# Weight-block sums for ten up-projection units made by DMA in DRAM during the attention, with the signs of the seven products on the token side

## The chip, the cores and the metric

The kernel runs on one core of one Trainium2 chip. The metric is device time in microseconds (us); lower is better. A core has five engines with queues of their own: TensorE (PE in the profile), VectorE (DVE), ScalarE (ACT), GpSimd (POOL) and SyncE (SP), which here only issues DMA transfers. Matrix products are written to PSUM banks; everything else lies in SBUF or in DRAM.

## The reference, cut to what matters

One layer of a diffusion backbone over 1024 tokens of width 1024, with 256 context tokens: modulated RMSNorm, a combined input projection that feeds neighbourhood attention (8 heads) and bidirectional retention (4 heads), gated merge, output projection and residual, and then a gated MLP with a centred convolution over three tokens:

```python
def _conv_ffn(h, w_up, conv_w, conv_b, w_down):
    u = h @ w_up                        # 1024 tokens x 5632 columns
    n = u.shape[1]
    pad = CONV_W // 2
    up = jnp.pad(u, ((0, 0), (pad, pad), (0, 0)))
    u = sum(up[:, i:i + n] * conv_w[i] for i in range(CONV_W)) + conv_b
    a, val = jnp.split(u, 2, axis=-1)
    return (jax.nn.silu(a) * val) @ w_down
```

All inputs, weights and the output are float32.

## The kernel before, in words

**Precision.** Each float32 operand is split in two parts of TensorE's reduced format: ACT copies the high part (`split`, L86), DVE subtracts it to get the low part (L87). A product is three matmuls: high by high, high by low, low by high. A weight block is a [128, 512] tile (256 KB); its two parts go in a `wc` tile, of which there are six.

**Stages**, in order of time: norms and first projections (to about 110 us of the profile), attention (to about 400 us), retention (to about 710 us), gates (to about 870 us), merge, output projection and second norm (to about 1125 us), up projection with convolution (to about 1525 us), down projection.

**Attention.** The loop runs over 34 iterations `i`: 32 units of one head pair and one block of 128 queries, and two to drain. Iteration `i` takes the scores of unit `i` (class `Unit`; its statistics tile `st` has three buffers), the transposes and value products of unit `i-1` and the output of unit `i-2`; between them `piece()` adds PE work from the projections of later pairs and of gates. In each iteration `ada_col2` multiplies one 512 KB block of `w_ada2` with the conditioning vector on DVE (L538); there is one buffer `aw` for it, and the load of the next block (L530) is issued behind that multiplication. That DVE instruction is pinned behind what was traced before it on its engine (`late` is `tc.keep_in_program_order`). POOL has nothing to do in this loop.

**Seven products.** The gates, the up projection and the down projection use a scheme of seven block products in place of eight (class `Seven`). For one block column of the up weights the four blocks are `a11, a12, a21, a22` (rows by column halves of the product's operand), and four sums of them are made on POOL (L1383 to L1386):

```python
pool.tensor_tensor(self.s1, self.a21, self.a22, ALU.add)
pool.tensor_tensor(self.s2, self.s1, self.a11, ALU.subtract)
pool.tensor_tensor(self.s3, self.a11, self.a21, ALU.subtract)
pool.tensor_tensor(self.s4, self.a12, self.s2, ALU.subtract)
```

The token side has four sums of its own, `T1` to `T4`: for the gates in `hx_sums`, for the up projection at the end of `norm_out`, from where they go to DRAM (`d_t`) and come back split in `comb` (tiles `T`). A unit has seven steps of 12 matmuls: `a11` by B11 into bank X, copied by ACT to `p1` (tile `pu`, L1408); `s2` by T2 into Y; `s1` by T1 into Z; `s3` by T3 into Y; `a12` by B21 into X; `a22` by T4 into Y; `s4` by B22 into Z. X and Y are the two halves of one PSUM tile `u`. DVE combines the banks (L1398, L1411, L1417).

**Up projection.** 22 units in the order `seq`; the first two (`PLAIN`) are made with plain products, and the other twenty (class `Up`, numbers 2 to 21) by seven products, each started about three and a half steps after the one before (`interleaved`). Behind every second unit stands the convolution (`conv`), whose result and its sums (tile `sa`, made on POOL, L1777) go to DRAM (`d_a`) for the down projection. The token sums' tiles, the weight blocks (`ur`, L1735) and the weight sums (`s`) share one ring of 12 tiles of [128, 512] (tag `r` of the pool `rp`). `load()` of a unit takes eight of them: four blocks loaded, four sums.

**Order.** The instructions of an engine are ordered when the program is built, by a planner that simulates the engines; each engine then runs its own list in that order and waits on semaphores. So an instruction at the head of an engine's list that waits holds up all behind it, and the order after a change is a new plan. SP's list holds all DMA issues.

Of the kernel before, what the change touches and what calls it, by code (L numbers as in the profile page):

```python
# [8 lines left out]
F32 = mybir.dt.float32  # L9
F32R = mybir.dt.float32r  # L10
AF = mybir.ActivationFunctionType
ALU = mybir.AluOpType
# [4 lines left out]
P = 128  # L17
# [15 lines left out]
NF = FF // P  # L33
# [7 lines left out]
def tile_hybrid_layer(ctx, tc: tile.TileContext, io, dbg=None):  # L41
    nc = tc.nc
    vec, act, pool, pe, sync = nc.vector, nc.scalar, nc.gpsimd, nc.tensor, nc.sync

    def sb(name, side, bufs=1):
        return tc.alloc_tile_pool(name=name, bufs=bufs, side=side, reuse_waits="tile")
# [4 lines left out]
    dram = tc.alloc_tile_pool(name="dram", bufs=1, space=DRAM)  # L51
    d_ona = dram.tile([GR, NJ, 8, NPAIR * P], F32, name="d_ona")
    d_oret = dram.tile([RH * 2, P, T], F32, name="d_oret")
    d_x1 = dram.tile([T, D], F32, name="d_x1")
    d_ada = dram.tile([32, P], F32, name="d_ada")
    d_gate = dram.tile([2 * KB, 2, P, 512], F32, name="d_gate")
    d_pn = dram.tile([KB, 2, P, 512], F32, name="d_pn")
    d_orr = dram.tile([RH * 2, P, T], F32, name="d_orr")
# [6 lines left out]
    cpool = sb("const", "left")  # L65
# [468 lines left out]
    late = tc.keep_in_program_order  # L534
# [6 lines left out]


    dec = cpool.tile([P, RH, 6], F32, name="dec")

    def load_ex():
        cst["lg"] = const("lg", [P, 2, RH])
        cst["ex"] = s0.tile([P, 5], F32, name="ex")
        sync.dma_start(cst["ex"], io["expo"])
# [456 lines left out]
    pieces = filler()  # L1005
# [3 lines left out]
    def piece():  # L1009
        next(pieces, None)  # L1010

    us = []
    for i in range(NPAIR * NJ + 2):
        live = i < NPAIR * NJ
        u1 = us[i - 1] if 1 <= i <= NPAIR * NJ else None
        u2 = us[i - 2] if i >= 2 else None
        if i == 0:
            ada_load()
        for n in (0, 1) if i == 1 else (i,) if 1 < i < 32 else ():
            ada_col2(n)  # L1020
        if u1:
            if u1.j == 0:
                u1.pair.values()
            u1.transp(0)
        piece()
        if u1:
            u1.transp(1)
        if live:
            pair = pairs[i // NJ]
            if i % NJ == 0 and i:  # L1030
                pair.load_bias()
            us.append(Unit(pair, i % NJ))
            us[i].scores()
        if u2:
            u2.output()
        if u1:
            u1.values()
        piece()
        piece()
    for _ in pieces:  # L1040
        pass
    pna.release()
    na.release()
    csp.release()
# [191 lines left out]
    NH = NF // 2  # L1236
# [105 lines left out]
    def hx_sums(k):  # L1342
        b = {}
        for i, half in ((0, 1), (0, 0), (1, 1), (1, 0)):
            kb, c0 = k + KH * i, half * 512
            b[i, half] = t = g_raw("b")
            late(pool.tensor_tensor(t, hxp(0, kb, c0, 512).bitcast(F32), hxp(1, kb, c0, 512).bitcast(F32), ALU.add))
        b11, b12, b21, b22 = b[0, 0], b[0, 1], b[1, 0], b[1, 1]
        for c, o, x, y in (("T1", b11, b12, b11), ("T3", b12, b22, b12), ("T2", b22, b22, b11), ("T4", b21, b21, b22)):
            late(vec.tensor_tensor(o, x, y, ALU.subtract))  # L1350
        yield
        for c, src in (("T2", b22), ("T1", b11), ("T3", b12), ("T4", b21)):
            split(hxT[c][0][:, k], hxT[c][1][:, k], src)
        yield
# [21 lines left out]
    class Seven:  # L1376
        loaded = False

        def load(self):
            self.loaded = True  # L1380
            self.a21, self.a22, self.a11, self.a12 = [self.raw(self.src[b, i]) for b, i in ((1, 0), (1, 1), (0, 0), (0, 1))]
            self.s1, self.s2, self.s3, self.s4 = (self.raw(None) for _ in range(4))
            pool.tensor_tensor(self.s1, self.a21, self.a22, ALU.add)  # L1383
            pool.tensor_tensor(self.s2, self.s1, self.a11, ALU.subtract)
            pool.tensor_tensor(self.s3, self.a11, self.a21, ALU.subtract)
            pool.tensor_tensor(self.s4, self.a12, self.s2, ALU.subtract)  # L1386

        def fetch(self, b, half):
            pass
# [4 lines left out]
            for k, (xh, xl) in enumerate(self.moving(c)):  # L1394
                open3(bank, w[:, 0, k * P : (k + 1) * P], w[:, 1, k * P : (k + 1) * P], xh, xl, first and k == 0, last and k == KH - 1)

        def add(self, b, half, bank, x):
            vec.tensor_tensor(self.dst(b, half), bank, x, ALU.add)  # L1398
            self.done(b, half)

        def step(self, n):
            if n == 0:
                if not self.loaded:
                    self.load()
                self.banks()
                self.p1, self.u2, self.u3 = (self.tmp() for _ in range(3))
                self.prod(self.X, self.a11, "B11", True, False)
                act.copy(self.p1, self.X)  # L1408
            elif n == 1:
                self.prod(self.Y, self.s2, "T2", True, False)  # L1410
                vec.tensor_tensor(self.u2, self.Y, self.p1, ALU.add)  # L1411
            elif n == 2:
                self.prod(self.Z, self.s1, "T1", True, False)
            elif n == 3:
                self.fetch(1, 1)
                self.prod(self.Y, self.s3, "T3", False, False)
                vec.tensor_tensor(self.u3, self.Y, self.p1, ALU.add)  # L1417
                self.add(1, 1, self.Z, self.u3)
            elif n == 4:
                self.fetch(0, 0)  # L1420
                self.prod(self.X, self.a12, "B21", False, True)
                self.c11()
            elif n == 5:
                self.fetch(1, 0)
                self.prod(self.Y, self.a22, "T4", False, True)
                self.add(1, 0, self.Y, self.p1)
            else:
                self.fetch(0, 1)
                self.prod(self.Z, self.s4, "B22", False, True)
                self.add(0, 1, self.Z, self.u2)  # L1430

    HALVES = {"B11": (0, 0), "B21": (KH, 0), "B22": (KH, 1)}

# [3 lines left out]
    class Gates(Seven):  # L1437
# [8 lines left out]
        def raw(self, src):  # L1446
            t = g_raw("wr")
            if src is not None:
                sync.dma_start(t, src)
            return t  # L1450
# [180 lines left out]
    op = sb("outp", "right")  # L1631
# [28 lines left out]
    def norm_out(tb, xr):  # L1660
        half, ts = tb // 4, slice((tb % 4) * P, (tb % 4 + 1) * P)
        if tb == 4:
            h2[1] = [(gtile(0, F32R, "h2h"), gtile(0, F32R, "h2l")) for _ in range(KB)]
        vr = op.tile([P, KB, P], F32, tag="v", bufs=2, name="v")
        if half:
            vo = op.tile([P, KB, P], F32, tag="vo", bufs=1, name="vo")
            sync.dma_start(vo, d_h[tb - 4])
        for kg in range(2):
            tp = po.tile([P, 4, P], F32, tag="t", bufs=2, name="tp2")
            for k in range(4):  # L1670
                pe.transpose(tp[:, k], xr[:, (kg * 4 + k) * P : (kg * 4 + k + 1) * P], ident)
            for k in range(4):
                kb = kg * 4 + k
                t = h2[half][kb]
                h_, l_ = (t[:, 0, ts], t[:, 1, ts]) if half == 0 else (t[0][:, ts], t[1][:, ts])
                a, sh = a2[:, kb : kb + 1], col[:, 24 + kb : 25 + kb]
                act.activation(h_, tp[:, k], AF.Identity, bias=sh, scale=a)
                v = vr[:, kb]
                vec.tensor_scalar(v, tp[:, k], a, sh, ALU.mult, ALU.add)  # L1679
                vec.tensor_tensor(l_, v, h_.bitcast(F32), ALU.subtract)  # L1680
        if half == 0:
            sync.dma_start(d_h[tb], vr)
            return

        (b11, b21), (b12, b22) = [(t[:, : KB // 2], t[:, KB // 2 :]) for t in (vo, vr)]
        vec.tensor_tensor(b11, b12, b11, ALU.subtract)
        vec.tensor_tensor(b12, b22, b12, ALU.subtract)
        vec.tensor_tensor(b22, b22, b11, ALU.subtract)
        vec.tensor_tensor(b21, b21, b22, ALU.subtract)
        for c, t in enumerate((b11, b22, b12, b21)):  # L1690
            sync.dma_start(d_t[c, tb - 4], t)

    xr = None
    for tb in range(NTB):
        nx = out_proj(tb)
# [93 lines left out]
    class Up(Seven):  # L1789


        def __init__(self, n, j):
            self.n, self.j = n, j
            self.src = {(b, i): io["w_up"][j, b, i] for b in range(2) for i in range(2)}

        def raw(self, src):
            return ur_load(src) if src is not None else rp.tile([P, 512], F32, tag="r", bufs=12, name="s")

# [28 lines left out]
    def down_source(j, c):  # L1827
# [3 lines left out]
        if x == "B":  # L1831
            return io["w_down"][n % 10 - 1, NH * (n // 10 - 1) + j]
        return d_a[{"A11": A11, "A12": A12, "A22": A22, "S1": S1, "S2": S2, "S3": S3, "S4": S4}[c], j]

    seq = [j + NH * i for j in range(NH) for i in range(2)]
    PLAIN = 2

    for n, j in enumerate(seq[:PLAIN]):
        us2 = []
# [8 lines left out]
    units = [Up(n, j) for n, j in enumerate(seq)]  # L1848
    for i, n in interleaved(PLAIN, NF):
        units[i].step(n)  # L1850
# [75 lines left out]
    for b in range(QB):  # L1926
        x, z = rows_of(b, 0), dw_tile("x2", NTB)
# [14 lines left out]
    for b in range(QB):  # L1942
        x, z = rows_of(QB + b, 1), dw_tile("x2", NTB)
# [8 lines left out]
    for b in range(QB):  # L1952
        tb = QB + b
        x, z = rows_of(tb, 0), dw_tile("z", 4)
# [132 lines left out]
```

## Time and profile before

| | us |
|---|---|
| median of three runs (1764.6 to 1767.07) | 1765.86 |
| profiled execution, first to last instruction (its span) | 1759.2 |
| the runs' median less that span | 6.7 |
| PE busy / DVE busy / ACT busy / POOL busy | 1726.0 / 1284.2 / 849.2 / 539.3 |

The profile gives no whole time of the profiled execution apart from its span; what lies around the span is taken as the difference to the median. In rows of the profile, L12 is line 12 of the kernel before; a name such as `wc<-ur,wc` says which tile is written from which. Rows of a timeline give the start in us, the duration in us, engine, line, operation, tiles and count, and in brackets how long the engine was idle before and what it waited for. SPq is SP's queue of DMA issues. A busy share is no proof of a bound: what counts is which engine others wait for in the stage at hand.

### The profile page before, as it was taken

The numbers are of one execution on the slowest core, as the hardware profiler recorded it, in microseconds if no ns is written. First come the engines' busy times: TensorE is split into PE (matmuls) and PEld (weight loads), VectorE is DVE, ScalarE is ACT, GpSimd is POOL, SyncE is SP. The second block draws the span as 40 slices with busy tenths as digits, with TensorE's granted clock in tenths as the row PEclk, the third lists the DMA queues.
The fourth block names the chain that finished last, engine by engine and source line by source line (L and its number), as shares of the span: only waits on it lengthen the run. The fifth ranks groups of instructions, "written<-read, shape, count | busy, mean of one in ns | idle before, by whom it ended". The sixth has DMA issues, their size and how long they took to land.

```text
span 1759.2 us, 24801 instructions
## 1 busy us (share of the span) xinstructions
PE 1726.0 (98%) x8405; PEld 1429.3 (81%) x8405; DVE 1284.2 (73%) x2454; ACT 849.2 (48%) x1826; POOL 539.3 (31%) x455
## 2 busy tenths in 40 slices
PE   8999999999999999999999999989999999999997
PEld 4688988888888888778888888778888888788886
DVE  4778887756776766777665557868899889875755
ACT  5666666653443434443444324534444444554444
POOL 1000000003334343555413300165555655211444
PEclk9999999999999999999999999999999999999999
DMA  9143334342231212677557733733322332586754
GB/s 348 61 130 125 95 117 147 117 133 87 73 108 43 72 42 68 203 238 239 200 199 268 246 143 132 254 108 102 108 90 92 118 120 90 170 296 192 239 162 162
DMA packets 139408, 261.10 MB, mean 148 GB/s; under 512 B 15856, under 2 KB 28304, under 8 KB 139280
## 3 DMA queue, kind: packets, MB, share of 16 engines
q1 hardware_dynamic: 139280, 259.51, 44.3%
q8 instruction: 66, 1.08, 0.3%
q14 instruction: 62, 0.51, 0.1%
HBM read 187.34 MB, written 69.48 MB: 146 GB/s over the span
## 4 chain that ended last, share of the span: by engine, by line
PE 43%; issue 6%; DVE 4%; POOL 3%; DMA 1%; ACT 1%; SPq 0%; POOLq 0%; ACTq 0%; DVEq 0%
PE u L1374 30%; PE y L1374 4%; PE pr L112 2%; PE pr L111 2%; PE pr L110 2%; PE om L122 1%; PE om L121 1%; PE om L123 1%; POOL x L1902 1%; DVE wc L87 0%; DVE b L1350 0%; DVE v L1679 0%; POOL pd L1939 0%; DVE hxT L87 0%; POOL x L1947 0%
## 5 line engine op out<-in xcount | busy, mean ns | idle before, releaser
L1374 PE MATMUL u<-T,wc 128*128 128x512 f32 x960 | 227.1, 392 | 5.1 <-ACT pu L1408 5.1
L1374 PEld LDWEIGHTS u<-T,wc 128*128 128x128 f32 x960 | 180.6, 189 | 45.7 <-ACT pu L1408 7.9
L1374 PE MATMUL y<-wc,ahl 128*128 128x512 f32 x924 | 210.6, 389 | 2.7 <-DVE wc L87 1.8
L1374 PEld LDWEIGHTS y<-wc,ahl 128*128 128x128 f32 x924 | 173.3, 188 | 39.7 <-DVE wc L87 2.5
L87 DVE TENSOR_TENSOR wc<-ur,wc 128x512 fp32r<-128x512 f32 x137 | 122.7, 897 | 65.8 <-ACT wc L86 65.8
L86 ACT CAST wc<-ur 128x512 fp32r<-128x512 f32 x137 | 85.0, 621 | 129.7 <-PE y L1374 72.3
L111 PE MATMUL mm<-low,wc 128*128 128x512 f32 (+1 forms) x328 | 124.0, 378 | 0.0
L1374 PE MATMUL u<-h2a,wc 128*128 128x512 f32 x480 | 112.3, 389 | 0.7 <-DVE pu L1417 0.7
L110 PE MATMUL mm<-hx,wc 128*128 128x512 f32 x264 | 107.4, 407 | 0.2 <-ACT wc L589 0.2
L1374 PEld LDWEIGHTS u<-h2a,wc 128*128 128x128 f32 x480 | 90.0, 188 | 19.8 <-DVE pu L1417 1.2
L112 PE MATMUL mm<-hx,wc 128*128 128x512 f32 x264 | 105.2, 399 | 0.0
L86 ACT CAST wc<-s 128x512 fp32r<-128x512 f32 x80 | 49.7, 623 | 93.2 <-PE u L1374 88.3
L123 PE MATMUL mm<-wc,low 128*128 128x512 f32 (+1 forms) x240 | 91.2, 380 | 0.0
L1374 PE MATMUL u<-hxT,wc 128*128 128x512 f32 x384 | 89.6, 389 | 0.0
L1508 POOL TENSOR_TENSOR col<-col,bcol 128x32 f32<-128x32 f32 x1 | 0.3, 253 | 280.7 <-DVE aw L538 280.7
L87 DVE TENSOR_TENSOR wc<-s,wc 128x512 fp32r<-128x512 f32 x80 | 83.5, 1046 | 3.8 <-ACT wc L86 3.4
L1374 PEld LDWEIGHTS u<-hxT,wc 128*128 128x128 f32 x384 | 72.1, 188 | 14.9
L87 DVE TENSOR_TENSOR wc<-raw,wc 128x512 fp32r<-128x512 f32 x92 | 68.0, 746 | 17.7 <-ACT wc L86 17.7
L121 PE MATMUL mm<-wc,hx 128*128 128x512 f32 x192 | 75.2, 392 | 0.6 <-ACT r L1105 0.6
L122 PE MATMUL mm<-wc,hx 128*128 128x512 f32 x192 | 75.2, 392 | 0.0
L1383 POOL TENSOR_TENSOR s<-ur 128x512 f32<-128x512 f32 x20 | 35.7, 1783 | 126.3 <-DVE wc L87 68.7
L86 ACT CAST wc<-raw 128x512 fp32r<-128x512 f32 x92 | 56.8, 621 | 33.0 <-PE pr L112 6.0
(393 smaller groups left out, 4671.3 us busy)
## 6 DMA issues: line engine op xcount, KB each, us to landing
ur<-in_w_up SPq DMA_DIRECT2D x80, 256.0 KB, 2.9
ur<-d_a SPq DMA_DIRECT2D x77, 256.0 KB, 3.1
aw<-in_w_ada SPq DMA_DIRECT2D x32, 512.0 KB, 3.3
pj<-in_w_down SPq DMA_DIRECT2D x44, 256.0 KB, 5.2
d_w<-pj SPq DMA_DIRECT2D x44, 256.0 KB, 2.0
d_a<-sa SPq DMA_DIRECT2D x44, 256.0 KB, 2.0
ur<-d_w SPq DMA_DIRECT2D x44, 256.0 KB, 3.8
d_a<-at SPq DMA_DIRECT2D x33, 256.0 KB, 2.7
```

Source lines behind the costliest of these rows:

```text
L86: act.copy(hi, src)
L87: (lo_eng or vec).tensor_tensor(lo, src, hi.bitcast(F32), ALU.subtract)
L110: pe.matmul(out, wh, xh, start=k == 0, stop=False)
L111: pe.matmul(out, wh, xl, start=False, stop=False)
L112: pe.matmul(out, wl, xh, start=False, stop=k == n - 1)
L121: pe.matmul(out, ah, bh, start=first, stop=False)
L122: pe.matmul(out, ah, bl, start=False, stop=False)
L123: pe.matmul(out, al, bh, start=False, stop=last)
L1374: pe.matmul(out, a, b, start=first and n == 0, stop=last and n == 2, skip_group_check=True)
L1383: pool.tensor_tensor(self.s1, self.a21, self.a22, ALU.add)
L1508: pool.tensor_tensor(col[:, 16:48], col[:, 16:48], bcol[:, 16:48], ALU.add)
L1902: pool.tensor_tensor(z, z, fg[:, gs(dh)], ALU.mult)
```

## The change

- A DRAM tensor `d_s` holds four sums of weight blocks for ten units of the up projection (numbers 2 to 11).
- During the attention loop POOL's DMA queue copies, for each of these units, four weight blocks from DRAM to `d_s` and adds four others to them by accumulating transfers, DRAM to DRAM, 256 KB each: 80 transfers in all. Each iteration that has a unit `i-1` first makes a one-column copy on POOL (`tick`) that reads the statistics of that unit, and then issues three transfers; `late` pins them to program order on POOL.
- Units 2 to 11 load seven tiles (three blocks, four sums) in the order in which they are used, and make no sums on POOL. Units 12 to 21 keep four loads and four sums.
- [...] The signs move to the token sums (`hx_sums`, `norm_out`) and to the combination of the banks; the number and the shapes of these instructions stay as they are. The down projection keeps its signs.

```diff
+    d_s = dram.tile([4, 10, P, 512], F32, name="d_s")
...
+    tick = cpool.tile([P, 1], F32, name="tick")
+    NH, PLAIN, PRE = NF // 2, 2, 10
+    seq = [j + NH * i for j in range(NH) for i in range(2)]
+
+    def up_sums():
+        def put(c, n, src, op=None):
+            kw = {} if op is None else dict(accum_op=op, max_dma_last_dim=8192)
+            late(pool.dma_start(d_s[c, n], src, **kw))
+
+        def w(n, b, i):
+            return io["w_up"][seq[PLAIN + n], b, i]
+
+        def begin(n):
+            for c, b, i in ((0, 1, 0), (2, 0, 0), (1, 0, 0), (3, 0, 1)):
+                yield put(c, n, w(n, b, i))
+
+        yield from begin(0)
+        for n in range(PRE):
+            nx = begin(n + 1) if n + 1 < PRE else iter(())
+            for c, src in ((0, w(n, 1, 1)), (2, w(n, 1, 0)), (1, d_s[0, n]), (3, d_s[1, n])):
+                yield put(c, n, src, ALU.add)
+                for _ in range(1):
+                    yield next(nx, None)
...
+    sums = up_sums()
     for i in range(NPAIR * NJ + 2):
...
         if u1:
             u1.values()
+            late(pool.tensor_copy(tick, u1.st[:, 14:15]))
+            for _ in range(3):
+                next(sums, None)
         piece()
         piece()
-    for _ in pieces:
-        pass
+    for it in (pieces, sums):
+        for _ in it:
+            pass
...
-        for c, o, x, y in (("T1", b11, b12, b11), ("T3", b12, b22, b12), ("T2", b22, b22, b11), ("T4", b21, b21, b22)):
-            late(vec.tensor_tensor(o, x, y, ALU.subtract))
+        for o, x, y, op in ((b11, b11, b12, ALU.subtract), (b12, b12, b22, ALU.subtract), (b22, b22, b11, ALU.add), (b21, b21, b22, ALU.subtract)):
+            late(vec.tensor_tensor(o, x, y, op))
...
-            pool.tensor_tensor(self.s2, self.s1, self.a11, ALU.subtract)
-            pool.tensor_tensor(self.s3, self.a11, self.a21, ALU.subtract)
-            pool.tensor_tensor(self.s4, self.a12, self.s2, ALU.subtract)
+            pool.tensor_tensor(self.s2, self.s1, self.a11, ALU.add)
+            pool.tensor_tensor(self.s3, self.a11, self.a21, ALU.add)
+            pool.tensor_tensor(self.s4, self.a12, self.s2, ALU.add)
...
-                vec.tensor_tensor(self.u2, self.Y, self.p1, ALU.add)
+                vec.tensor_tensor(self.u2, self.p1, self.Y, ALU.subtract)
...
-                vec.tensor_tensor(self.u3, self.Y, self.p1, ALU.add)
-                self.add(1, 1, self.Z, self.u3)
+                vec.tensor_tensor(self.u3, self.Y, self.p1, ALU.subtract)
+                self.add(1, 1, self.u3, self.Z, ALU.subtract)
...
+        def load(self):
+            n = self.n - PLAIN
+            if n >= PRE:
+                return super().load()
+            self.loaded = True
+            self.a11, self.s2, self.s1, self.s3, self.a12, self.a22, self.s4 = map(ur_load, (self.src[0, 0], d_s[1, n], d_s[0, n], d_s[2, n], self.src[0, 1], self.src[1, 1], d_s[3, n]))
```

More of the change, by code (lines that the diff above doesn't have):

```diff
@@ L1395, in prod, with add @@
                 open3(bank, w[:, 0, k * P : (k + 1) * P], w[:, 1, k * P : (k + 1) * P], xh, xl, first and k == 0, last and k == KH - 1)
-        def add(self, b, half, bank, x):
-            vec.tensor_tensor(self.dst(b, half), bank, x, ALU.add)
+        def add(self, b, half, x, y, op):
+            vec.tensor_tensor(self.dst(b, half), x, y, op)
             self.done(b, half)
@@ L1425, in step @@
                 self.prod(self.Y, self.a22, "T4", False, True)
-                self.add(1, 0, self.Y, self.p1)
+                self.add(1, 0, self.Y, self.p1, ALU.subtract)
             else:
@@ L1429, in step @@
                 self.prod(self.Z, self.s4, "B22", False, True)
-                self.add(0, 1, self.Z, self.u2)
+                self.add(0, 1, self.Z, self.u2, ALU.add)
     HALVES = {"B11": (0, 0), "B21": (KH, 0), "B22": (KH, 1)}
@@ L1685, in norm_out @@
         (b11, b21), (b12, b22) = [(t[:, : KB // 2], t[:, KB // 2 :]) for t in (vo, vr)]
-        vec.tensor_tensor(b11, b12, b11, ALU.subtract)
-        vec.tensor_tensor(b12, b22, b12, ALU.subtract)
-        vec.tensor_tensor(b22, b22, b11, ALU.subtract)
+        vec.tensor_tensor(b11, b11, b12, ALU.subtract)
+        vec.tensor_tensor(b12, b12, b22, ALU.subtract)
+        vec.tensor_tensor(b22, b22, b11, ALU.add)
         vec.tensor_tensor(b21, b21, b22, ALU.subtract)
@@ L1833, in down_source @@
         return d_a[{"A11": A11, "A12": A12, "A22": A22, "S1": S1, "S2": S2, "S3": S3, "S4": S4}[c], j]
-    seq = [j + NH * i for j in range(NH) for i in range(2)]
-    PLAIN = 2
     for n, j in enumerate(seq[:PLAIN]):
```

## The prediction

> **What bounds the kernel now.** I read the shares of busy time first, then who PE waited for, then the timeline of the one long wait, engine by engine.
>
> ```profile
> span 1759.2 us, 24801 instructions
> PE 1726.0 (98%) x8405; PEld 1429.3 (81%) x8405; DVE 1284.2 (73%) x2454; ACT 849.2 (48%) x1826; POOL 539.3 (31%) x455
> ```
> ```profile
> 1200.00:1480.00 280.00, 280.00 (x1231) 230.24 (x1230) 252.89 (x251) 127.46 (x177) 155.84 (x89) 1.00 0.31 102
> ```
> ```profile
> PE u L1374 <- ACT pu L1408: 5.1, 1, 5.1
> ...
> PE u L1374 <- DVE pu L1417: 0.7, 1, 0.7
> ```
>
> The second fence is one window of the up projection: span, PE, PE's weight loads, DVE, ACT, POOL, granted clock, DMA share, GB/s. PE is busy for 280.00 of 280 us there although DVE is at 90% and POOL at 56%. So the 155.84 us that POOL works beside it are hidden, and taking sums from POOL gains nothing in that stretch. What can be gained is PE's idle time. The longest single wait of the whole span is 5.1 us, on the first unit that uses the weight sums:
>
> ```profile
> 1147.63 2.88 PE L1374 MATMUL u<-h2a,wc 128*128 128x512 f32 x12
> 1150.35 1.07 PE L1374 MATMUL u<-T,wc 128*128 128x512 f32 x4
> 1156.57 9.09 PE L1374 MATMUL u<-T,wc 128*128 128x512 f32 x32 [5.15 <-ACT pu L1408]
> 1165.49 5.60 PE L1374 MATMUL u<-h2a,wc 128*128 128x512 f32 x24
> ```
> ```profile
> 1156.50:1166.00 9.50, 9.43 (x35) 7.68 (x36) 6.57 (x9) 2.09 (x5) 6.64 (x5) 0.82 0.44 140
> ```
>
> Twelve matmuls from 1147.63 to 1150.35 are 227 ns each; the 32 behind the wait take 8.92 us instead of 32 x 0.227 = 7.25. These 1.67 us are a clock that was lowered: granted 0.82 over 9.5 us, (1 - 0.82) x 9.5 = 1.7. The wait costs 5.15 + 1.67 = 6.82 us together.
>
> [...]
>
> Why did PE wait? Three queues hand the delay on:
>
> ```profile
> 1133.35 2.47 SPq L1735 DMA_DIRECT2D ur<-in_w_up  x4
> 1140.20 0.33 SPq L1766 DMA_DIRECT2D d_a<-at  x1
> 1148.02 10.13 SPq L1735 DMA_DIRECT2D ur<-in_w_up  x8
> ```
> ```profile
> 1139.52 5.42 POOL L1383 TENSOR_TENSOR s<-ur 128x512 f32<-128x512 f32 x1 [33.12 <-DMA ur<-in_w_up]
> 1145.02 1.72 POOL L1384 TENSOR_TENSOR s<-s,ur 128x512 f32<-128x512 f32 x1
> 1146.70 1.29 POOL L1385 TENSOR_TENSOR s<-ur 128x512 f32<-128x512 f32 x1
> ```
> ```profile
> 1140.10 3.69 DVE L87 TENSOR_TENSOR T<-ur,T 128x512 fp32r<-128x512 f32 x6
> ```
> ```profile
> 1152.85 0.62 ACT L86 CAST wc<-ur 128x512 fp32r<-128x512 f32 x1 [4.21 <-DMA ur<-in_w_up]
> ...
> 1155.93 0.58 ACT L1408 COPY pu<-u 128x512 f32<-128x512 f32 x1
> ```
>
> The four blocks of unit 2 are issued at 1133.35. POOL's first sum takes 5.42 us beside a busy DVE, the others follow, and the third ends at 1147.99. It is the last reader of unit 2's first block, so the ring's tile comes free there, and SP issues the first loads of unit 3 at 1148.02. ACT's list has unit 3's first split ahead of the copy of bank X (`pu`): it idles 4.21 us for that load, does three more things, and copies X at 1155.93 to 1156.51. PE's T2 products, which write the other half of the same PSUM tile, start at 1156.57. So the wait that names ACT ends a chain that begins with POOL's sums.
>
> **The change part by part.**
>
> *The sums of units 2 to 11 leave POOL.* Per unit:
>
> ```profile
> L1383 POOL TENSOR_TENSOR s<-ur 128x512 f32<-128x512 f32 x20 | 35.7, 1783 | 126.3 <-DVE wc L87 68.7 <-DMA ur<-in_w_up 43.8 <-DVE at L1760 10.6
> L1384 POOL TENSOR_TENSOR s<-s,ur 128x512 f32<-128x512 f32 x20 | 27.4, 1369 | 32.8 <-issue 28.2 <-DVE wc L87 2.8 <-DMA ur<-in_w_up 1.5
> L1385 POOL TENSOR_TENSOR s<-ur 128x512 f32<-128x512 f32 x20 | 44.1, 2204 | 9.4 <-DVE wc L87 9.4
> L1386 POOL TENSOR_TENSOR s<-ur,s 128x512 f32<-128x512 f32 x20 | 41.4, 2072 | 1.5
> ```
>
> 1.78 + 1.37 + 2.20 + 2.07 = 7.4 us, for ten units 74 us of POOL. All of it lay beside a full PE, except at the first unit. There the chain is cut: unit 2's seven tiles and the first five of unit 3 fill the ring's 12, and wait only for the token sums' splits, the last of which ends on DVE at 1140.10 + 3.69 = 1143.8. Unit 3's first tile is its `a11`; issued by about 1141 and landed 3 to 4 us later (1148.02 to 1152.85 was 4.8 with eight behind one another), it is there before the copy of X is due at 1150.4. What is late next is the copy itself: PE's end of `a11`, 0.58 us of copy, against 4 x 0.227 = 0.91 us of T1 products that the plan put between. The residue is between 0 and 1.0 us (no T1 product between); I take 0.3, since four were there before. Gain: 6.82 - 0.3 = 6.5 us.
>
> *Three more loads in each of ten units.* 30 issues by SP and 7.9 MB in about 190 us are 41 GB/s on top of 102, at a DMA share of 0.31. SP waits for tiles there, not for time. With seven tiles per unit instead of eight the ring reaches further ahead. Cost 0; without that cover a load of 3 to 5 us would show on PE, at a unit each.
>
> *Signs.* The same DVE and POOL instructions in number and shape, one sign or operand order different: 0.
>
> *`tick` and 80 transfers on POOL's queue in the attention.* POOL is free:
>
> ```profile
> 369.90 0.25 POOL L1508 TENSOR_TENSOR col<-col,bcol 128x32 f32<-128x32 f32 x1 [280.66 <-DVE aw L538]
> ```
>
> Nobody waits for POOL here, except that `tick` now reads `st`: with three buffers, DVE's scores of unit i+3 wait for unit i's `tick`. Behind `tick` in POOL's list stand three issues, and an accumulation waits for the copy or accumulation whose bytes it needs. In the generator's order the closest pair has one issue between, so POOL stands for most of an accumulation's landing about twice in eight transfers. A transfer's landing is not shown for DRAM to DRAM; the nearest rows from below and above:
>
> ```profile
> d_w<-pj SPq DMA_DIRECT2D x44, 256.0 KB, 2.0
> ...
> x<-in_w_ada1g SPq DMA_DIRECT2D x16, 512.0 KB, 8.4
> ```
>
> I take 5 us, twice a plain load and more, as it reads two sources. An issue on POOL costs between 0.33 us (SP's, in the row below) and 5.42 (POOL held up by DVE, above); I take 1.3, the undisturbed sum of 1.29. Eight issues and two waits are 8 x 1.3 + 2 x 4 = 18.4 us. One iteration lasts
>
> ```profile
> L538 DVE SCALAR_TENSOR_TENSOR aw<-aw,cs x32: 1215/1217/1228, 111.6 to 368.5; 128x1024 f32<-128x1024 f32 x32
> ...
> DMA to landing us min/median/max: 3.1/3.3/4.1
> ```
>
> (368.5 - 111.6) / 31 = 8.3 us, and eight transfers have 8/3 of it, 22 us. So POOL keeps up, not by much.
>
> *What these transfers take from others.* In the attention:
>
> ```profile
> 110.00:400.00 290.00, 289.14 (x1779) 253.57 (x1778) 223.08 (x635) 186.43 (x554) 0.70 (x3) 1.00 0.39 124
> ```
> ```profile
> q1 hardware_dynamic: 17328, 35.69, 38.4%
> ```
> ```profile
> 920.00:960.00 40.00, 40.00 (x178) 33.13 (x177) 20.90 (x30) 17.41 (x30) 9.90 (x8) 1.00 0.83 289
> ```
>
> 35.69 MB took 38.4% of 290 us, 3.1 us of all 16 engines per MB. 10.5 MB of copies are 33 us, 10.5 MB of accumulations 33 to 66: together 28 to 43% of the 28 iterations (232 us) that hold them. The share rises from 0.39 to 0.67 to 0.82. In the last row, in the merge, PE stayed full at 0.83. The transfer with least room is `aw`, one buffer, next in line on DVE:
>
> ```profile
> 181.99 0.33 SPq L530 DMA_DIRECT2D aw<-in_w_ada  x1
> ```
> ```profile
> 187.91 1.23 DVE L538 SCALAR_TENSOR_TENSOR aw<-aw,cs 128x1024 f32<-128x1024 f32 x1
> ```
>
> Here 5.9 us lie between issue and use; on average 8.3 - 1.3 - 0.1 = 6.9. Landing now takes 3.3; I expect 4 to 5.5, inside that. Bounds for the attention: 0, and the two prices below; I take 0.2 us for small collisions. A gain there is excluded up to PE's 0.86 idle us in the window.
>
> **Sum.** 6.82 saved, less 0.3 and 0.2: 6.3 us. The span goes from 1759.2 to 1752.9; the 6.7 us between span and median stay, and the median goes from 1765.86 to 1759.5.
>
> **The rivals.**
>
> *The wait comes back in the same place.* The new plan may put another wait ahead of the copy of X (unit 2's `s3`, a late store on SP). A gap of 3.5 us would still lower the clock: 3.5 + 1.67 lost, 1.65 saved, 1764.2. For it: the order is planned anew. Against it: all seven loads can be issued 4 us before they are needed.
>
> *`aw` lands too late.* It decides at a landing of 6.9 us on average. The 8.4 us above, in the first 40 us of the span, would hold DVE, pinned to its order, for 1.5 us in 28 iterations: 42 us slower, 1801.5; a landing of 7.4 gives 14 us, 1773.5. For it: DVE is busy for 223 of 290 us, so PE cannot be kept fed by working ahead for long. Against it: 4.1 was the longest here.
>
> *POOL falls behind.* It decides at 22 us for eight transfers, 2.7 each with waits. At 3.2 each, three take 9.6, 1.3 us more than an iteration; 28 x 1.3 = 36 us, less the two iterations (16.6) that three buffers of `st` forgive: 20 slower than forecast, 1779. For it: POOL's sum of 1.29 us took 5.42 beside DVE.
>
> [...] If every issue were held like the sum of 5.42 us, three would take 16.3 us and the attention would last (16.3 - 8.3) x 28 - 16.6 = 207 us longer.
>
> **How the numbers follow.** About 0.2% (3.5 us) is what a measurement of this kernel can tell from no change. Stall gone and attention undisturbed: 0.66, time 1759.5. Wait back in place: 0.11, same. Late `aw`: 0.13, and POOL behind: 0.10, both slower. The low end takes residue, collisions and the 0.7 us wait for DVE away, and the scatter of the runs: 1765.86 - 6.82 - 0.7 - 1.3 = 1757.0. The high end takes in the mild form of the slower cases (`aw` at 7.4 us), 1774; about 0.16 lies above it.
>
> **What would show it right or wrong.** Right: PE's row of 5.1 us behind `pu` is gone, no clock below 1.00 from 1130 to 1500 us, POOL's L1383 to L1386 count 10 for `s`, PE still busy for 289 of 290 us in the attention. Wrong: DVE's L538 has idle time ahead that a DMA ended; DVE or PE waits for POOL's `tick`; POOL's issues stand more than 2.7 us apart at the median; the up projection starts with another gap of over 1 us.

## The result and the profile after

| | median us (runs) | ratio to before, 95% interval | span of the profiled run |
|---|---|---|---|
| before | 1765.23 (4) | | 1759.2 |
| after | 1780.95 (4, 1777.76 to 1784.52) | 1.0092 [1.0076, 1.0107] | 1775.7 |

The changed kernel is 0.9% slower. The profiled run of it took 1777.76 us, 2.1 us more than its span, while before's profiled span lies 6.0 us below its median, so the spans differ by 16.5 us and the medians by 15.7. In every later run that lists both, the time is 1.7 to 2.1 us above the span, so before's profile must be of an execution some 4 us faster than its median, and each comparison of spans with it carries that.

The head of the page after, and two windows of it that answer to those of before (span, PE, weight loads, DVE, ACT, POOL, granted clock, DMA share, GB/s):

```profile
span 1775.7 us, 25019 instructions
PE 1738.2 (98%) x8405; PEld 1429.8 (81%) x8405; DVE 1263.0 (71%) x2454; ACT 850.1 (48%) x1826; POOL 520.6 (29%) x527
```
```profile
1216.00:1496.00 280.00, 280.00 (x1211) 226.95 (x1210) 231.59 (x246) 126.25 (x174) 112.52 (x67) 1.00 0.36 117
...
110.00:400.00 290.00, 281.67 (x1728) 245.78 (x1728) 216.54 (x615) 181.13 (x538) 57.65 (x113) 0.99 0.68 187
```

POOL lost 43 us of the up projection's 280-us window (155.84 to 112.52) and DVE 21, and PE was full in both. But in the new window PE started 1211 matmuls in 280 us at full clock, where it started 1231 before. In the attention PE is busy for 281.67 of 290 us, where it was 289.14. Both are losses, at two places. What the change was to remove is gone. PE's and ACT's timelines after, at the first unit with weight sums:

```profile
1163.95 2.91 PE L1403 MATMUL u<-h2a,wc 128*128 128x512 f32 x12
1166.70 8.56 PE L1403 MATMUL u<-T,wc 128*128 128x512 f32 x36
1175.10 5.61 PE L1403 MATMUL u<-h2a,wc 128*128 128x512 f32 x24
```
```profile
1166.90 0.59 ACT L1437 COPY pu<-u 128x512 f32<-128x512 f32 x1 [1.02 <-PE u L1403]
```

The 4 + 32 `u<-T` matmuls are now one row without a gap: the copy `pu` ran at 1166.90, and PE did not wait for it.

A stage table shows where the spans part. I take the first and last start of a matmul group in each trace: the attention from the first scores (`sl`) to the last `tq`; the middle (retention, output projection, gate products, merge) up to the first `u<-T`; the up projection from there to the first `y`; then the down projection's matmuls to the last `y`.

| us | attention | middle | up | down |
|---|---|---|---|---|
| before | 282.3 | 765.5 | 378.5 | 222.0 |
| after | 293.0 | 771.7 | 378.2 | 222.0 |
| after, `tick` inside the pad | 289.9 | 767.5 | 371.0 | 224.0 |
| before, moved by an unused `tick` | 282.1 | 770.6 | 383.9 | 223.3 |

The third and fourth rows are the first two experiments; they already separate the two losses. Each row is one profile: the same work in the same stage still scatters by 1 to 2 us between profiles.

### The profile page after: what moved, and what is told of

Its sections match the earlier page's. It is cut to its first block, busy times and chain, and to the rows that moved or that the text cites. A ratio compares the mean times of both kernels' runs of the same rounds, so it can differ in the third digit from the quotient of the medians.

```text
span 1775.7 us, 25019 instructions
## 1 busy us (share of the span) xinstructions
PE 1738.2 (98%) x8405; PEld 1429.8 (81%) x8405; DVE 1263.0 (71%) x2454; ACT 850.1 (48%) x1826; POOL 520.6 (29%) x527
## 4 chain that ended last, share of the span: by engine, by line
PE 80%; issue 6%; DMA 5%; DVE 4%; POOL 3%; ACT 2%; SPq 0%; POOLq 0%; ACTq 0%; DVEq 0%
PE u L1403 30%; PE y L1403 4%; PE mm L123 4%; PE mm L124 4%; PE mm L122 4%; PE mm L111 3%; PE mm L113 3%; PE mm L112 3%; DMA aw<-in_w_ada 2%; PE om L122 2%; PE om L124 2%; PE om L123 2%; PE pr L113 2%; PE pr L112 2%; PE pr L111 2%
## 5 line engine op out<-in xcount | busy, mean ns | idle before, releaser
L1403 PE MATMUL u<-T,wc 128*128 128x512 f32 x960 | 230.5, 396 | 0.0
L88 DVE TENSOR_TENSOR wc<-ur,wc 128x512 fp32r<-128x512 f32 x177 | 142.4, 807 | 76.0 <-ACT wc L87 75.9
L87 ACT CAST wc<-ur 128x512 fp32r<-128x512 f32 x177 | 109.5, 620 | 174.9 <-PE u L1403 96.2
L1806 POOL TENSOR_TENSOR sa<-at 128x512 f32<-128x512 f32 x22 | 39.0, 1772 | 209.4 <-DVE at L1792 161.4
L112 PEld LDWEIGHTS mm<-low,wc 128*128 128x128 f32 x328 | 63.2, 193 | 7.0
L1063 POOL COPY tick<-st 128x1 f32<-128x1 f32 x32 | 5.9, 185 | 212.7 <-DVE st L486 212.7
L88 DVE TENSOR_TENSOR wc<-wr,wc 128x512 fp32r<-128x512 f32 x56 | 52.6, 945 | 18.1 <-ACT wc L87 16.6
```

Source lines behind the costliest of these rows:

```text
L87: act.copy(hi, src)
L88: (lo_eng or vec).tensor_tensor(lo, src, hi.bitcast(F32), ALU.subtract)
L112: pe.matmul(out, wh, xl, start=False, stop=False)
L1063: late(pool.tensor_copy(tick, u1.st[:, 14:15]))
L1403: pe.matmul(out, a, b, start=first and n == 0, stop=last and n == 2, skip_group_check=True)
L1806: pool.tensor_tensor(prev[c], x, y, o)
```

## The experiments

**First theory (placement).** The changed kernel adds one tile of 4 bytes, `tick`, on the left side of SBUF. It is padded to 32 bytes, so that every later tile on the left (`wc`, `raw`, `hx`, `h2a`, `orr`, `ahl`) lies 32 bytes higher, and no tile on the right (`T`, `hxT`, `h2h`, `ona`, `mh`, `wo`) moves. The rows above contain the effect: after, 36 `u<-T` matmuls take 1175.10 - 1166.70 = 8.40 us, 233.3 ns each. **Second theory (late loads).** The transfers make `aw` late in the attention. **Rival to both:** the new order of the up projection, or its signs, costs the time.

*The changed kernel without its address shift.*

```diff
-    cpool.tile([P, 24], F32, name="pad")
+    left_pad = cpool.tile([P, 24], F32, name="pad")
...
-    tick = cpool.tile([P, 1], F32, name="tick")
+    tick = left_pad[:, 0:1]
```

> The changed kernel, with the one-column tile of tick laid inside a padding tile that is there anyway, so that no tile's address moves. Placement theory: the 4-byte tile moved all tiles on the left side of SBUF by 32 bytes against those on the right side, and matmuls whose two operands come from different sides took 0.2334 us from start to start instead of 0.2267; that goes, about 13 us: span 1775.7 to about 1763, time about 1768 (ratio to before 1.001 to 1.003), token-sum matmuls (T, hxT) back at 0.2267. Rival, the new signs or the values that they make are what slows these matmuls: they stay at 0.2334 and the time at about 1780 (1.009). Both: the attention stays 10 us longer.

Measured: 1767.07 us median, 1.0017 [1.0006, 1.0028], span 1764.2. Of the 15.7 us that the change costs, 13.9 are gone with an edit that leaves every instruction and transfer in place. The attention stays longer than before, but by 7.6 us and not by the 10 expected.

*The kernel before with nothing but the address shift.*

```diff
     dec = cpool.tile([P, RH, 6], F32, name="dec")
+    cpool.tile([P, 1], F32, name="tick")
```

> The kernel before, with one unused one-column tile allocated where the change puts tick; no instruction is added. Placement theory: 12 to 14 us slower than before (ratio about 1.007 to 1.008), the T, hxT and second-half h2 matmuls at 0.2334 from start to start, and the 5.15 us wait at the first unit of the up projection stays. Rival, signs: no difference to before (1.000).

Measured: 1773.38 us, 1.0049 [1.0037, 1.0062], span 1771.1. A tile that nobody reads or writes costs 0.5%. The direction is as expected, the size is not: 8.1 us over the 1765.29 of before beside it, instead of 12 to 14. Rows of PE's timeline of before, after, and this kernel; the second row of each gives the start of what follows:

```profile
1247.34 8.32 PE L1374 MATMUL u<-T,wc 128*128 128x512 f32 x36
1255.50 0.39 PE L1374 MATMUL u<-h2h,wc 128*128 128x512 f32 x1
```
```profile
1258.41 8.56 PE L1403 MATMUL u<-T,wc 128*128 128x512 f32 x36
1266.81 0.40 PE L1403 MATMUL u<-h2h,wc 128*128 128x512 f32 x1
```
```profile
1253.09 8.56 PE L1375 MATMUL u<-T,wc 128*128 128x512 f32 x36
1261.49 0.40 PE L1375 MATMUL u<-h2h,wc 128*128 128x512 f32 x1
```

The same 36 matmuls, with no wait and at full clock, take 8.16, 8.40 and 8.40 us: 226.7 and 233.3 ns. Over the whole trace I add, for each pair of matmuls that start 222 to 240 ns apart, what the step exceeds 226.7 ns: 6.8 us before, 20.3 after, 6.5 with `tick` in the pad, 20.2 in before with the unused tile. So the placement adds 13.4 to 13.5 us of slower steps. They fall on the products that read one operand on the left and one on the right (`u<-T`, `u<-hxT`, `u<-h2h`, `u<-h2l`, `pn<-ona`, `om<-wc`; 233.2 to 234.0 ns in the means after); `pr<-orr` and `y<-wc,ahl`, with both operands on the left, keep 226.7 ns. No wait shows them, since PE is not idle in these rows.

In time, the slower steps cost the kernel before less than their sum. One reason is in its trace: it still has the wait for `pu`, and that wait gets shorter. It was 5.1 us, and with the unused tile it is

```profile
PE u L1375 <- ACT pu L1409: 3.9, 1, 3.9
```

The up projection grows by 5.4 us there, although its steps grow by 7.8. In the changed kernel, which has no such wait, moving `tick` into the pad was worth 13.9 us. That the shorter wait is the whole of the difference is not shown.

*What about the placement decides?* Both sides were shifted next. The theory then was that two operands with the same remainder modulo 64 go fast.

```diff
     dec = cpool.tile([P, RH, 6], F32, name="dec")
+    cpool.tile([P, 1], F32, name="tick")
...
-    edge.tile([P, 24], F32, name="pad")
+    edge.tile([P, 32], F32, name="pad")
```

> As e2 (the kernel before, left side moved by 32 bytes), with the tiles of the right side moved by 32 bytes too (a padding tile there of 32 columns in place of 24). If what counts is how the two operands of a matmul lie to each other: T, hxT and the second half of h2 are back at 0.2267 us, time as before (ratio 0.999 to 1.001). Rival, an address that is no multiple of 64 bytes is slow by itself: all of them are slow, 1773 or more (1.005 and above).

Measured: 1775.57 us, 1.0063 [1.0051, 1.0075], span 1774.0; the sum over 226.7 ns is 20.1 us. That theory fell. The right side grows downward, so 8 more columns put it 32 bytes lower, and the distance between the sides was 64 bytes less than before. Two theories were left: the start address itself, or the distance. Two kernels tell them apart. The first puts every tile 32 bytes higher, at before's distances; the second moves only the left side, by 64 bytes, at before's remainders modulo 64:

```diff
     dec = cpool.tile([P, RH, 6], F32, name="dec")
+    cpool.tile([P, 1], F32, name="tick")
...
-    edge.tile([P, 24], F32, name="pad")
+    edge.tile([P, 16], F32, name="pad")
```

> The kernel before, with the unused tick tile of 4 bytes (every tile on the left of SBUF 32 bytes higher) and the right-hand pad tile cut from 24 to 16 columns (every tile on the right 32 bytes higher too): all distances between left and right tiles are those of before, and all start addresses have the remainder 32 modulo 64. Theory 1, the start address of an operand modulo 64 decides: the step of the products u<-T and hxT is 0.2333 us as in the run with only tick added, the time 1.005 of before or a little more (1773 to 1776 us). Theory 2, the distance between the weight's and the activation's tiles decides: step 0.2267 us, time 1.000 (1765 us). The run with both sides moved and the distance changed by 64 bytes stayed at 0.2333 us, which fits both.

```diff
-    cpool.tile([P, 24], F32, name="pad")
+    cpool.tile([P, 40], F32, name="pad")
```

> The kernel before with the left pad tile widened from 24 to 40 columns: every tile on the left lies 64 bytes higher, the right side stays, no work is changed. Theory 1 (start address modulo 64): nothing changes, step 0.2267 us, time 1.000 (1765 us). Theory 2 (distance between the sides): step 0.2333 us, time 1.005 (1773 us).

Measured: with all tiles moved alike 1764.86 us, 1.0004 [0.9995, 1.0013], span 1763.1; with the left side 64 bytes higher 1773.03 us, 1.0061 [1.0048, 1.0073], span 1772.8. PE's timeline of the one and of the other:

```profile
1249.60 8.32 PE L1375 MATMUL u<-T,wc 128*128 128x512 f32 x36
1257.76 0.39 PE L1375 MATMUL u<-h2h,wc 128*128 128x512 f32 x1
```
```profile
1255.04 8.56 PE L1374 MATMUL u<-T,wc 128*128 128x512 f32 x36
1263.43 0.40 PE L1374 MATMUL u<-h2h,wc 128*128 128x512 f32 x1
```

8.16 and 8.39 us. In these runs the step goes with the distance between the weight's and the activation's tiles, not with where either starts: 226.7 ns at before's distances, also with every tile 32 bytes higher, and 233.1 ns with the left side alone 64 bytes higher. In before the distances of the products named above are multiples of 256 bytes; shortened by 32 bytes (233.3 ns) or by 64 (233.1 ns) they were slow. Which other distances are fast was not tried, and why they matter stays open. Distance is not the only cause of a longer step: in before's merge `om<-wx,mh` steps at 232.2 ns where `om<-wc,mh` steps at 226.7, and half of the former, like many `mm` products in the attention and the retention (`mm<-hx,wc` 230.5 ns in the mean), read operands a multiple of 256 bytes apart.

*The transfers alone.* Before's signs, loads and sums, with `tick` (in the pad) and all 80 transfers in the attention. `d_s` and `up_sums` are as in the change and are left out here.

```diff
...
             u1.values()
+            late(pool.tensor_copy(tick, u1.st[:, 14:15]))
+            for _ in range(3):
+                next(sums, None)
```

> The kernel before (old signs, old up projection with its sums on POOL), with tick (inside the padding) and the 80 transfers in the attention; their results are not used. Transfer theory: the attention is 10 us longer, the rest as before, 1775 to 1777 (ratio 1.005 to 1.007), and the wait of DVE's L538 for the load of aw is there. Rival, the attention's loss is the placement or the new plan and not the transfers: 1765 to 1768 (below 1.002).

Measured: 1775.70 us, 1.0061 [1.0048, 1.0074], span 1772.5: about 10 us for transfers that nobody reads. The attention lasts 291.6 us instead of 282.3. The up projection lasts 379.2 us, as long as before, and still has its wait: the first of the two rows below.

*The signs alone.* No `tick`, no transfers; all units load four tiles and make their sums, with the new signs, under which all four weight sums are additions.

```diff
-            late(pool.tensor_copy(tick, u1.st[:, 14:15]))
-            for _ in range(3):
-                next(sums, None)
...
-    NH, PLAIN, PRE = NF // 2, 2, 10
+    NH, PLAIN, PRE = NF // 2, 2, 0
...
-    sums = up_sums()
+    sums = iter(())
```

> The kernel before with the new signs alone: four additions on POOL for all twenty units, new signs on the token side and in the combinations, no tick, no transfers, no address moved. Expected: no difference (ratio 0.999 to 1.001), matmuls at 0.2267, the 5 us wait still there. Rival, the signs cost or bring time by themselves: outside 0.998 to 1.002.

Measured: 1763.95 us, 0.9999 [0.9990, 1.0008]: the signs cost nothing, and the wait is there (second row):

```profile
PE u L1403 <- ACT pu L1437: 4.7, 1, 4.7
```
```profile
PE u L1400 <- ACT pu L1434: 5.5, 1, 5.5
```

So the wait goes when the first units' sums leave POOL, and not through signs or through traffic. These units then also take seven tiles of the ring and not eight, and load them in the order of use; the runs do not separate this from POOL's time.

*Are the attention's 10 us late `aw` loads?* The waits and the tile `aw` of the kernel after:

```profile
DVE aw L539 <- DMA aw<-in_w_ada: 9.8, 8, 3.6
```
```profile
DMA to landing us min/median/max: 3.1/4.1/9.3
```

DVE waited eight times for `aw`, 9.8 us in all. The longest case, from the timeline after:

```profile
121.22 1.87 POOL L552 DMA_DIRECT2D d_s<-in_w_up  x3 [0.25 <-issue]
```
```profile
123.33 0.53 SPq L531 DMA_DIRECT2D aw<-in_w_ada  x1
...
131.67 1.23 DVE L539 SCALAR_TENSOR_TENSOR aw<-aw,cs 128x1024 f32<-128x1024 f32 x1 [3.57 <-DMA aw<-in_w_ada]
...
133.61 0.42 DVE L515 TENSOR_TENSOR rs<-R,rs 128x256 f32<-128x256 f32 x1
...
134.09 0.66 PE L494 MATMUL ptp<-ident,P 128*128 128x128 f32 x4 [3.06 <-DVE rs L515]
```
```profile
120.00:160.00 40.00, 36.90 (x228) 31.96 (x226) 28.97 (x85) 24.68 (x74) 8.82 (x18) 0.96 0.67 177
```

POOL issues three transfers at 121.22; SP's load of `aw` follows at 123.33 and lands 8.3 us later, DVE stands 3.57 us for it, what DVE has behind it (`rs`) is late, and PE waits 3.06 us for `rs`. The last row shows the price beside the wait: the granted clock over these 40 us is 0.96. It was 0.74 from 134.50 to 135.00, 0.50 from there to 138.00 and 0.92 to 139.00: 0.13 + 1.50 + 0.08 = 1.7 us of lost clock behind a wait of 3.06 us, as much as before lost behind its wait of 5.15 (1.67). Before's trace has the same clock at the end of a wait of 3.3 us (`tpn` for `ona`): 0.50 from 719.60 to 722.60. The gap of 3.5 us in the prediction's first rival lies between these waits. The test is to give `aw` a second buffer and to load two iterations ahead:

```diff
-        w = na.tile([P, D], F32, tag="aw", bufs=1, name="aw")
+        w = na.tile([P, D], F32, tag="aw", bufs=2, name="aw")
...
-        if i + 1 < 32:
+        if i + 2 < 32:
             ada_load()
...
         if i == 0:
             ada_load()
+            ada_load()
```

> As e1, with two buffers for aw, loaded two iterations ahead. If DVE's wait for aw, pinned in its order, is what costs the attention 10 us: that wait goes, the attention is back to within 2 us, and the time is about 1758 to 1760 (ratio 0.996), below before. Rival, the transfers slow all other loads or DVE and POOL as well: the attention keeps most of its 10 us and the time is that of e1, about 1768.

This is on top of `tick` in the pad, with all 80 transfers. Measured: 1758.74 us, 0.9959 [0.9948, 0.9971], span 1757.3. The attention's window of the kernel with `tick` in the pad, and then of this one:

```profile
110.00:400.00 290.00, 283.26 (x1739) 246.77 (x1738) 218.15 (x620) 183.01 (x544) 58.42 (x114) 1.00 0.69 189
```
```profile
110.00:400.00 290.00, 288.46 (x1769) 251.44 (x1768) 222.82 (x633) 186.00 (x555) 58.49 (x115) 1.00 0.70 195
```

The DMA share did not fall (0.69 and 0.70), loads of `aw` still land after up to 8.6 us, and no wait for `aw` is left; PE is busy for 288.46 us instead of 283.26, and the attention lasts 283.7 us instead of 289.9. So it was the lateness of this one load, not the traffic as such. The control, two buffers in the kernel before:

> The kernel before with two buffers for the attention's weight piece aw, loaded two iterations ahead; no transfers, no other signs. My theory, that the transfers made these loads late and that nothing else in the attention waits for them: 1.000 of before (1764 to 1766 us), the end of the attention where it was. A rival: the loads already cost something in the kernel before, and two buffers are a gain by themselves: the attention ends 1 to 2 us sooner, 0.9990.

Measured: 1764.94 us, 1.0008 [0.9999, 1.0017], attention 282.7 us. The second buffer is no gain by itself.

*How many units are needed?* With `tick` in the pad and one `aw` buffer, only the first unit's sums, 8 transfers:

```diff
-    NH, PLAIN, PRE = NF // 2, 2, 10
+    NH, PLAIN, PRE = NF // 2, 2, 1
```

> As e1 (tick inside the padding), but only the first of the ten units gets its sums by DMA: 8 transfers in three iterations in place of 80 in 28; the other nineteen make theirs on POOL. If the whole gain is the 5 us wait of PE at the first unit, it stays whole: no PE wait behind the copy pu, and with little left of the attention's loss (0 to 5 us: the 8 transfers fall in the short first iterations, where aw has least room) the time is 1758 to 1763 (ratio 0.996 to 0.999). Rival, units 2 to 10 also bring time in the up projection: the up projection is longer than in e1 by some us.

Measured: 1761.89 us, 0.9989 [0.9981, 0.9998]. The up projection's 378.5 us become 372.1, nearly all of the gain (371.0 with ten) from one unit of ten. The attention still loses 5 us (287.5): `aw` is late twice, both times in the first 30 us of it. So the same 8 transfers were put one to an iteration, from the 13th on:

```diff
-            late(pool.tensor_copy(tick, u1.st[:, 14:15]))
-            for _ in range(3):
-                next(sums, None)
+            if i >= 12:
+                late(pool.tensor_copy(tick, u1.st[:, 14:15]))
+                next(sums, None)
```

> As e5, with the 8 transfers one to an iteration from iteration 12 on. With room for aw in each iteration: no wait of DVE's L539 for aw, the attention within 1 us of before, the wait at the first unit gone: about 1758.5 (ratio 0.996). If a single transfer beside aw is enough to hold DVE: 1760 or more.

Measured: 1759.52 us, 0.9972 [0.9963, 0.9982]; attention 283.3 us, no wait for `aw`. The waits came out as expected; the time is 1 us above the expected 1758.5, and 0.996 lies just outside the interval. Both remedies together:

> The changed kernel with tick inside the pad tile, one unit's sums (8 transfers, one per iteration from the 13th on), and two buffers for aw. If what is left of the attention's loss in the run with one late unit (3.3 us) is aw coming late, it goes: attention at before's end to +1 us, time 0.9955 to 0.9962 (1757 to 1758.5 us), equal to or below the run with ten units and two buffers (0.9959). If it is queueing of other loads, or of the vector engine's work behind the copies that pace the transfers, it stays at 0.9972.

Measured: 1758.74 us, 0.9971 [0.9962, 0.9980], span 1756.2, attention 283.0 us. The second buffer adds nothing where the transfers are few and late: the first of the two expected outcomes missed. What looked like a rest of 3.3 us with one late unit and one buffer was mostly there before the attention begins: in that profile the first scores start 2.4 us later than in before's. The interval of both remedies together overlaps that of ten units with two buffers, so which of the two is the better is not settled; each is faster than the kernels before and after.

## Why the prediction was wrong

The forecast was 1759.5 us and faster; the kernel took 1780.95. By the stage table the terms of its sum are these.

**Right: the stall and its size.** Forecast 6.5 us. The up projection without the address shift takes 371.0 us instead of 378.5, and in the four other kernels that cut the chain 371.5 to 372.8: a gain of 5.7 to 7.5 us. PE's row has no gap behind the copy at 1166.90, so there is no residue. The wait did not come back. That taking sums from POOL gains next to nothing at the units behind the first was right as well: one unit gives 372.1 us, ten give 371.0.

**Right: signs 0, more loads 0, POOL keeps up.** The signs alone left the time at 0.9999, and the up projection is no longer with ten units of three more loads than with one. POOL's groups, the landings and POOL's waits after:

```profile
L552 POOL DMA_DIRECT2D d_s<-in_w_up x60 | 39.4, 736 | 5.9 <-issue 5.9
L552 POOL DMA_DIRECT2D d_s<-d_s x20 | 16.7, 835 | 17.4 <-DMA d_s<-d_s 15.0 <-issue 2.4
```
```profile
d_s<-in_w_up POOLq DMA_DIRECT2D x60, 256.0 KB, 5.1
```
```profile
POOL tick L1063 <- DVE st L486: 212.7, 31, 21.2
```

An issue took 0.74 to 0.84 us on average (estimate 1.3) and 1.11 at the longest, a transfer landed after 5.1 us at the median (estimate 5), and POOL waited 212.7 us for the next iteration. No issue was held as the sum of 5.42 us was, beside a DVE that was busy for 216.54 of the attention window's 290 us. The DMA share rose to 0.68, the low end of the 0.67 to 0.82 forecast.

**Wrong: 0.2 us for small collisions in the attention; it was 10.7.** (It was 7.6 and 9.3 in the two other kernels with all 80 transfers and one buffer.) This is the rival of the late `aw`, taken at 0.13, and its mechanism is what happened. The step that failed is the comparison of an expected landing with an average room, 6.9 us, and one row of 5.9. A load can be late in any single iteration, so the shortest rooms and the longest landings decide, and the trace of before had shorter rooms. DVE's and SP's rows at the beginning of the attention, before:

```profile
116.10 1.22 DVE L538 SCALAR_TENSOR_TENSOR aw<-aw,cs 128x1024 f32<-128x1024 f32 x1
121.48 1.23 DVE L538 SCALAR_TENSOR_TENSOR aw<-aw,cs 128x1024 f32<-128x1024 f32 x1
128.00 1.23 DVE L538 SCALAR_TENSOR_TENSOR aw<-aw,cs 128x1024 f32<-128x1024 f32 x1
```
```profile
112.90 4.79 SPq L530 DMA_DIRECT2D aw<-in_w_ada  x2
123.19 0.53 SPq L530 DMA_DIRECT2D aw<-in_w_ada  x1
```

The rooms there are 116.10 - 112.90 = 3.2 us for the first of the two loads and 128.00 - 123.19 = 4.8 for the third; the landing alone took 3.1 to 4.1. The forecast landing of 4 to 5.5 us was right for the median (4.1) and not for the longest (9.3). The second longest of the eight waits came from such a landing, 212.72 - 203.43 = 9.3 us:

```profile
203.43 0.33 SPq L531 DMA_DIRECT2D aw<-in_w_ada  x1
```
```profile
212.72 1.23 DVE L539 SCALAR_TENSOR_TENSOR aw<-aw,cs 128x1024 f32<-128x1024 f32 x1 [2.37 <-DMA aw<-in_w_ada]
```

The rival was priced as if every load were late by the same amount. Eight late loads of 32 and one drop of the clock were enough.

**Wrong: nothing was put down for `tick` as a tile.** The sum counted what `tick` executes and not what it moves: 13.5 us of slower steps, 13.9 us of time, the larger of the two losses and without a row of idle time. No rival had it. From the traces, the change's terms are -7.5 (up projection, without the shift) + 10.7 (attention) + 13.5 (steps) = +16.7 us, against 16.5 between the spans; that they meet so closely is partly luck, as single profiles scatter by more. The times say the same without a trace: `tick` in the pad gives back 13.9 us and the second buffer 8.3 more, which ends 6.5 us below before, and 13.9 + 8.3 - 6.5 = 15.7.

## What to carry to other kernels

A new tile of 4 bytes moved what is allocated behind it by 32 bytes and cost 13.9 us: compare the steps between the starts of back-to-back matmuls of the same shape before and after an edit (a count of matmuls per full window shows it), and put small tiles into existing padding. Where transfers are added beside other work, look for the single-buffered load with the shortest time between issue and use, iteration by iteration, and give that one a second buffer. Where a chain is cut to remove one wait, cut it at that place alone: one unit of ten, late in the attention, gave nearly what ten units gave.

## What was not expected of the hardware

- The step of the back-to-back 128x512 matmuls `u<-T` was 226.7 or 233.3 ns depending on the distance between the tiles of their two operands; moving all tiles by 32 bytes together changed nothing (1.0004), moving the left side alone by 32 or 64 bytes cost 0.5 to 0.6% (1.0049, 1.0061).
- A load of 512 KB that lands in 3.3 us at the median before landed in 4.1 at the median and 9.3 at the longest beside DRAM-to-DRAM transfers, at a mean DMA share of 0.68.
- Copies and accumulating transfers, DRAM to DRAM and 256 KB each, cost POOL 0.74 to 0.84 us per issue on average, 1.11 at the longest, beside a DVE that was busy for three quarters of the time (216.54 of 290 us).
